# The gated linear recurrence ordered by halves of four heads, one VectorE multiply per level, constants staged in the 4 KB pool

## The chip, the core and the metric

The kernel runs on one core of a Trainium2 chip. The metric is the device time of one execution in microseconds (us). TensorE is called PE (its weight loads PEld), VectorE DVE, ScalarE ACT, GpSimd POOL, and SyncE SP.

## What is computed

A stack of three blocks over 256 rows of 1024 features in float32: an attention layer with a top-k mask (`dsa`) and a swiglu network, a gated linear recurrence (`hgrn`) and a swiglu network, and a third block. The change touches the recurrence. Cut to what matters:

```python
def hgrn2_mixer(x, lb, w_in, g_norm, w_o):
    q, f, i, g = split(x @ w_in)                 # four times 1024 columns, 8 heads of 128
    q = silu(q); fg = lb + (1 - lb) * sigmoid(f); k = 1 - fg; logf = log(fg)
    o = chunk_gated_linear(q, k, i, logf)        # S_t = diag(f_t) S_{t-1} + k_t v_t^T ; o_t = S_t^T q_t
    o = rms_norm(o, g_norm) * silu(g)
    return o @ w_o
```

## The kernel before

The 256 rows are two tiles of 128, t = 0 and 1. Every weight matrix is streamed once. SP loads a unit of 128 x 1024 numbers (512 KB) into one of 4 `raw` buffers, ACT rounds it to `rhi` (L174), DVE, or POOL for the keys in `ON_POOL`, takes the rest `rlo` (L176, L181), and a product is three matmuls (L210 to L212). One projection of 512 columns for one t is 24 matmuls of 128x512; its weights are four units, used for both t.

The strings `DSA`, `HEAD0` and so on, `HGRN` and `MIX` write out the order of the steps. A scheduler at build time takes that order as priorities and fixes each engine's own order from it, so instructions of neighbouring steps interleave. Each pool of buffers hands out whichever buffer is free.

In the first swiglu network (`ffn`), three small steps are laid beside chunks 2 and 3 (`ASIDE`). The last of them, `hgrn_consts` (L696), loads three constants over POOL's DMA queue into three tiles of the `raw` pool: `sel` (used by 8 matmuls at L705 to spread the bound `lb`), `lev` (the sums of the recurrence's levels, cast at L709), and `msk`, `suf`, `id64` together (cast or copied at L713 to L717). Their DVE, ACT and PE instructions are kept behind the work traced before them (`later`).

`hgrn` (L721): `project` (P.kind half.t) makes f, q, i, g by halves n of 512 columns, that is four heads. `evac` applies sigmoid, silu or a copy. `logs` (l.t) takes the logarithm over both halves, `turned` (t.t) turns q and k of all eight heads into `qT` and `kT`, `state` (S) builds the state that t = 1 reads. `pair` (p.t.i) does the recurrence of heads 2i and 2i+1 within 128 rows. It goes through 7 levels (8 for t = 1), two at a time: PE sums logarithms (L807, L808), ACT takes Exp (L810), then the late part of each block of rows is multiplied by q (L817) and the early part by k (L819; levels 2 and 5 on POOL, by `h_k2` and `h_k5`). PE multiplies them (L824, L830), and DVE copies the results by a mask (L835) into `blocks`, then into `attn` (L224). The output product is L846 and L848. Every second pair ends with `norm_heads` (L292 to L296). `gated` (g.t.n) multiplies by silu(g) and the norm's weight (L867 to L870) and turns the result; `out` (o.n.t) is the last projection, for which both halves of row tile t must be gated.

Pools named below: `w4` has 10 buffers of 4 KB per partition, `raw` 4, `rhi` and `rlo` 9 each. The logarithms lie in `rhi`/`rlo` tiles (`lfh`, `lfl`).

Of the kernel before, what the change touches and what calls it, by code (L numbers as in the profile page):

```python
# [10 lines left out]
F32 = mybir.dt.float32  # L11
F32R = mybir.dt.float32r
# [75 lines left out]
class Net:  # L88
# [631 lines left out]

    def hgrn(self, XT, dst):  # L721
        nc, ins = self.nc, self.ins
        w_in, w_o = ins["hgrn_w_in"][0], ins["hgrn_w_o"][0]
        lb, lev, msk, suf, id64, gn = self.hgrn_held
        fg, q, v, sg, qT, kT, lf, dg = ([None, None] for _ in range(8))

        def evac(kind, t, n, a):
            c = slice(n * 512, (n + 1) * 512)
            dst = {"f": fg, "q": q, "i": v, "g": sg}[kind]
            if n == 0:  # L730
                dst[t] = (self.g4 if kind in "ig" else self.w4)(name=kind)
            o = dst[t][:, c]
            if kind in "ig":
                self.copy(o, a, "h_" + kind)
            elif kind == "q":
                nc.scalar.activation(o, a, AF.Silu)
            else:

                nc.scalar.activation(o, a, AF.Sigmoid)
# [4 lines left out]
        def logs(t):  # L744

            lf[t] = (self.tile("rhi", (P, D), F32R, "lfh"), self.tile("rlo", (P, D), F32R, "lfl"))
            for n in range(2):
                c = slice(n * 512, (n + 1) * 512)
                x = self.w2(t, name="lf")
                nc.scalar.activation(x, fg[t][:, c], AF.Ln)  # L750
                self.halves(lf[t][0][:, c], lf[t][1][:, c], x)
                nc.vector.tensor_scalar(fg[t][:, c], fg[t][:, c], -1.0, 1.0, ALU.mult, ALU.add)

        def turned(t):

            dg[t] = self.sm(t, 8, name="dg")
            qT[t], kT[t] = self.w4((P, 8, P), name="qT"), self.w4((P, 8, P), name="kT")
            for n in range(2):
                c, b = slice(n * 512, (n + 1) * 512), slice(4 * n, 4 * n + 4)
                qk = self.w2(t, (P, 4, P), name="qk")  # L760
                nc.gpsimd.tensor_tensor(qk.rearrange("p h d -> p (h d)"), q[t][:, c], fg[t][:, c], ALU.mult)
                nc.vector.tensor_reduce(dg[t][:, b], qk, AX.X, ALU.add)
                self.copy(qT[t][:, b, :], self.blocksT(self.cols(q[t], 4 * n, 4), "hT"), "h_qT")
                self.copy(kT[t][:, b, :], self.blocksT(self.cols(fg[t], 4 * n, 4), "hT"), "h_kT")

        S = [None]

        def state():

            S[0] = self.w4((P, 8, P), name="S")  # L770
            for n in range(2):
                c = slice(n * 512, (n + 1) * 512)
                a = self.bank("hE")
                nc.tensor.matmul(a, suf, lf[0][0][:, c], start=True, stop=False)
                nc.tensor.matmul(a, suf, lf[0][1][:, c], start=False, stop=True)
                e = self.w2(0, name="e")
                nc.scalar.activation(e, a, AF.Exp)
                nc.vector.tensor_mul(e, e, fg[0][:, c])
                a = self.bank("hS", (P, 4, P))
                for j in range(4):  # L780
                    nc.tensor.matmul(
                        a[:, j, :], e[:, j * P : (j + 1) * P], v[0][:, n * 512 + j * P : n * 512 + (j + 1) * P],
                        start=True, stop=True,
                    )
                self.copy(S[0][:, n * 4 : n * 4 + 4, :], a, "h_S")

        part = lambda y, l, s: y.rearrange("p j (b s e) -> p j b s e", s=2, e=64 >> l)[:, :, :, s, :]

        def pair(t, i):

            hs = slice(2 * i, 2 * i + 2)
# [9 lines left out]
            for l0 in range(0, 7 + t, 2):  # L801
                m = min(2, 7 + t - l0)
                x = self.bank("hx%d" % (l0 // 2), (P, 2, 2, P), name="lx")
                rhs = lev[:, l0 * P : (l0 + m) * P].rearrange("p (l n) -> p l n", l=m)
                for j in range(2):
                    c = slice((2 * i + j) * P, (2 * i + j + 1) * P)
                    nc.tensor.matmul(x[:, j, :m, :], lf[t][0][:, c], rhs, start=True, stop=False)  # L807
                    nc.tensor.matmul(x[:, j, :m, :], lf[t][1][:, c], rhs, start=False, stop=True)  # L808
                e = self.w2(l0 // 2 % 2, (P, 2, 2, P), name="e")
                nc.scalar.activation(e[:, :, :m, :], x[:, :, :m, :], AF.Exp)  # L810
                for l in range(l0, l0 + m):
                    y = e[:, :, l - l0, :]
                    if l == 7:
                        nc.vector.tensor_mul(y, y, qT[t][:, hs, :])
# [28 lines left out]
            for j in range(2):  # L843
                h = 2 * i + j
# [29 lines left out]
        def out(n, t):
            if not rows:
# [429 lines left out]
MIX = (  # L1305
# [79 lines left out]
```

## Time and profile before

| | |
|---|---|
| median of 3 runs | 1156.86 us (1151.27 to 1157.37) |
| profiled execution, own time | 1154.16 us |
| its span | 1152.4 us |
| DMA | 187.33 MB, mean 163 GB/s |

Start times in all rows are us from the span's start. A window's row gives its length, then the busy time of each engine with its count of instructions, the granted clock of PE as a share of full speed (1.00 is 2.4 GHz, 0.50 is 1.2 GHz), the DMA engines' share, and GB/s. In a timeline, the bracket behind an instruction is how long its engine had been idle, and who ended that. Matmuls are pipelined, so the distance from one start to the next counts, not the length.

### The profile page before, as it was taken

To read this page: it belongs to the slowest core of one execution; us is meant where nothing else is said; L and a number is where in the kernel's file an instruction comes from. 1 tells how busy PE (TensorE), PEld (TensorE's weight loads), DVE (VectorE), ACT (ScalarE), POOL (GpSimd) and SP (SyncE) were. 2 spreads that over 40 slices of the span, in tenths; PEclk is the share of its full clock that TensorE was granted. 3 is DMA by queue.
4 is the path that set the end of the run, shared out by engine and by line. 5 is a ranking of instruction groups with operands and counts; after the bars stand their busy time and mean duration, and the time that the engine had idled before them with its cause. 6 is when DMAs were issued, how large, how long until landed. Compare 5 with 4: busy or idle time off the path is not lost.

```text
span 1152.4 us, 15343 instructions
## 1 busy us (share of the span) xinstructions
PE 1106.6 (96%) x5724; PEld 903.0 (78%) x5724; DVE 697.3 (61%) x1061; ACT 583.9 (51%) x832; POOL 224.3 (19%) x336
## 2 busy tenths in 40 slices
PE   8779999999999999999999999999999999999997
PEld 6546888878888777788888887887788878888886
DVE  6986755535566677875545486446655547454542
ACT  5656455525467466444444346763546456453441
POOL 2800620000432223200000022534100181000000
PEclk9989999999999899999999999999999999999999
DMA  8420756547445342365656545663554446566541
GB/s 250 159 85 5 243 166 229 182 119 255 146 146 173 103 145 77 119 214 180 218 183 192 175 131 174 207 159 102 164 192 146 146 146 225 174 222 202 171 140 37
DMA packets 98458, 187.33 MB, mean 163 GB/s; under 512 B 9400, under 2 KB 26952, under 8 KB 98384
## 3 DMA queue, kind: packets, MB, share of 16 engines
q1 hardware_dynamic: 94816, 176.28, 48.1%
q0 software_dynamic: 2864, 9.45, 2.5%
q8 instruction: 45, 0.74, 0.3%
q10 hardware_dynamic: 704, 0.62, 0.2%
q14 instruction: 29, 0.24, 0.1%
HBM read 185.28 MB, written 1.05 MB: 162 GB/s over the span
## 4 chain that ended last, share of the span: by engine, by line
PE 81%; DVE 8%; POOL 4%; DMA 3%; issue 2%; ACT 2%; SPq 0%; POOLq 0%; DVEq 0%; ACTq 0%
PE a L210 15%; PE a L211 15%; PE a L212 15%; PE y L211 8%; PE y L210 8%; PE y L212 8%; PE t L236 3%; POOL rlo L181 2%; DVE rlo L176 1%; PE lv L830 1%; DMA raw<-in_ffn_w_up_dram 1%; DMA raw<-in_ffn_w_gate_dram 1%; DVE m L381 1%; ACT rhi L174 1%; PE L L538 1%
## 5 line engine op out<-in xcount | busy, mean ns | idle before, releaser
L176 DVE TENSOR_TENSOR rlo<-raw,rhi 128x1024 fp32r<-128x1024 f32 (+4 forms) x306 | 370.2, 1215 | 216.3 <-ACT rhi L174 204.8
L174 ACT ACTIVATE rhi<-raw 128x1024 fp32r<-128x1024 f32 (+3 forms) x338 | 352.7, 1047 | 242.8 <-PE y L212 75.5
L210 PE MATMUL a<-rhi,xh 128*128 128x512 f32 (+4 forms) x840 | 318.6, 379 | 3.4 <-ACT sil L625 1.8
L211 PE MATMUL a<-rlo,xh 128*128 128x512 f32 (+4 forms) x840 | 316.7, 377 | 0.2 <-DVE rlo L176 0.2
L212 PE MATMUL a<-rhi,xl 128*128 128x512 f32 (+4 forms) x840 | 315.4, 376 | 0.0
L210 PEld LDWEIGHTS a<-rhi,xh 128*128 128x128 f32 x840 | 158.7, 189 | 32.1 <-ACT xh L174 2.0
L211 PEld LDWEIGHTS a<-rlo,xh 128*128 128x128 f32 x840 | 158.8, 189 | 27.8 <-DVE rlo L176 0.6
L212 PEld LDWEIGHTS a<-rhi,xl 128*128 128x128 f32 x840 | 158.8, 189 | 27.4
L181 POOL TENSOR_TENSOR rlo<-raw,rhi 128x256 fp32r<-128x256 f32 x128 | 99.2, 811 | 179.8 <-ACT rhi L174 179.7
L210 PE MATMUL y<-rhi,hth 128*128 128x512 f32 x264 | 104.7, 396 | 0.5 <-ACT hth L174 0.5
L212 PE MATMUL y<-rhi,htl 128*128 128x512 f32 x264 | 103.2, 391 | 0.0
L211 PE MATMUL y<-rlo,hth 128*128 128x512 f32 x264 | 102.9, 390 | 0.0
L210 PE MATMUL y<-rhi,xh 128*128 128x512 f32 (+2 forms) x152 | 59.1, 390 | 3.1 <-ACT rhi L174 3.1
L257 POOL TENSOR_SCALAR rv<-mv 128x1 f32<-128x1 f32 x10 | 7.2, 716 | 272.0 <-DVE mv L266 271.8
L211 PE MATMUL y<-rlo,xh 128*128 128x512 f32 (+2 forms) x152 | 59.0, 388 | 1.0 <-POOL rlo L181 0.6
L212 PE MATMUL y<-rhi,xl 128*128 128x512 f32 (+2 forms) x152 | 58.6, 387 | 0.0
L174 ACT ACTIVATE hth<-t 128x512 fp32r<-128x512 f32 (+1 forms) x36 | 20.1, 558 | 75.6 <-PE t L236 75.6
L210 PEld LDWEIGHTS y<-rhi,hth 128*128 128x128 f32 x264 | 49.6, 188 | 10.7 <-ACT hth L174 1.1
L212 PEld LDWEIGHTS y<-rhi,htl 128*128 128x128 f32 x264 | 49.5, 188 | 10.6
L211 PEld LDWEIGHTS y<-rlo,hth 128*128 128x128 f32 x264 | 49.6, 188 | 9.7
L631 DVE TENSOR_TENSOR sil<-a,sil 128x512 f32<-128x512 f32 (+1 forms) x36 | 23.2, 643 | 51.1 <-PE a L212 51.0
L625 ACT ACTIVATE sil<-a 128x512 f32<-128x512 f32 (+1 forms) x36 | 20.2, 561 | 58.9 <-PE a L212 58.8
(412 smaller groups left out, 1435.0 us busy)
## 6 DMA issues: line engine op xcount, KB each, us to landing
raw<-in_ffn_w_gate_dram SPq DMA_DIRECT2D x44, 512.0 KB, 4.7
raw<-in_ffn_w_up_dram SPq DMA_DIRECT2D x44, 512.0 KB, 4.7
raw<-in_ffn_w_down_dram SPq DMA_DIRECT2D x44, 512.0 KB, 4.6
raw<-in_hgrn_w_in_dram SPq DMA_DIRECT2D x32, 512.0 KB, 4.5
raw<-in_w_in_dram SPq DMA_DIRECT2D x24, 512.0 KB, 4.4
raw<-in_w_ffn_gate_dram SPq DMA_DIRECT2D x22, 512.0 KB, 4.3
raw<-in_w_ffn_up_dram SPq DMA_DIRECT2D x22, 512.0 KB, 4.6
raw<-in_w_ffn_down_dram SPq DMA_DIRECT2D x22, 512.0 KB, 4.5
```

What stands on the lines that cost most here:

```text
L174: self.nc.scalar.activation(hi, src, AF.Copy)
L176: self.nc.vector.tensor_sub(lo, src, hi.bitcast(F32))
L181: eng.tensor_sub(lo[:, c], src[:, c], hi[:, c].bitcast(F32))
L210: mm(out, xh, wh, start=start, stop=False)
L211: mm(out, xh, wl, start=False, stop=False)
L212: mm(out, xl, wh, start=False, stop=stop)
L236: self.nc.tensor.transpose(tp[:, j, :], b, self.ident)
L381: e2.tensor_tensor(m2, v[:, :, ::-1, :], s[:, None, :, :].to_broadcast(sh), ALU.mult)
L538: nc.tensor.matmul(L[:, j : j + 2, :], qT[t][:, g * 4 + (h0 + j) // 2, :], kT[:, g, :, :nk], start=False, stop=j == per - 2,)
L625: nc.scalar.activation(sil[ci, t][:, :cn], a[:, :cn], AF.Silu)
L631: nc.vector.tensor_mul(sil[ci, t][:, :cn], a[:, :cn], sil[ci, t][:, :cn])
L830: nc.tensor.matmul(lv[64 * c : 64 * c + 64, l - l0, j, :32], y, late, start=True, stop=True)
```

## The change

Five things are changed.

- `hgrn_consts` stages its three loads in tiles of `w4` instead of `raw`.
- f and q of one half and one t share a 4 KB tile, and so do the turned k and q (`QK[t, n]`, k first). `logs`, `turned` and `state` work on one half n, and the logarithms of one half, both t, lie in one `lfh`/`lfl` tile.
- In `pair`, each level has one DVE multiply over all 256 elements (two heads of 128): `asked(l)` is an access pattern over `QK` that takes k for the early and q for the late part of each block. The multiplies of levels 2 and 5 thereby leave POOL.
- `ON_POOL` loses `h_k2` and `h_k5`.
- The order `HGRN` goes through heads 0 to 3 for both t, then heads 4 to 7, with projections between the pairs.

```diff
-        raw = lambda: self.tile("raw", (P, 1024), F32, "raw")
-        sel = self.load(raw()[0:8, :], self.const("sel", 8)).rearrange("p (a b) -> p a b", a=8)
+        stage = [self.w4(name="stage") for _ in range(3)]
+        sel = self.load(stage[0][0:8, :], self.const("sel", 8)).rearrange("p (a b) -> p a b", a=8)
...
-        nc.vector.tensor_copy(lev, self.load(raw(), self.const("lev")))
+        nc.vector.tensor_copy(lev, self.load(stage[1], self.const("lev")))
...
-        both = self.load(raw()[:, : n + P + 64], self.consts[:, o : o + n + P + 64])
+        both = self.load(stage[2][:, : n + P + 64], self.consts[:, o : o + n + P + 64])
...
+                both = self.w4(name="fq")
+                fg[t, n], q[t, n] = both[:, :512], both[:, 512:]
...
+        def logs(t, n):
+            if n not in lf:
+                lf[n] = (self.tile("rhi", (P, 2, 512), F32R, "lfh"), self.tile("rlo", (P, 2, 512), F32R, "lfl"))
...
+        def turned(t, n):
...
+            both = QK[t, n] = self.w4((P, 2, 4, P), name="QK")
...
+            self.copy(both[:, 1, :, :], self.blocksT(self.cols(q[t, n], 0, 4), "hT"), "h_qT")
+            self.copy(both[:, 0, :, :], self.blocksT(self.cols(fg[t, n], 0, 4), "hT"), "h_kT")
...
+            def asked(l):
+                x = QK[t, n][:, 0, j0 : j0 + 2, :]
+                w = 64 >> l
+                return bass.AP(tensor=x.tensor, offset=x.offset, ap=[x.ap[0], [P, 2], [2 * w, 64 // w], [4 * P + w, 2], [1, w]])
...
-                    nc.vector.tensor_mul(part(y, l, 1), part(y, l, 1), part(qT[t][:, hs, :], l, 1))
-                    eng = nc.gpsimd if "h_k%d" % l in ON_POOL else nc.vector
-                    eng.tensor_tensor(part(y, l, 0), part(y, l, 0), part(kT[t][:, hs, :], l, 0), ALU.mult)
+                    y = y.rearrange("p j (b s e) -> p j b s e", s=2, e=64 >> l)
+                    nc.vector.tensor_tensor(y, y, asked(l), ALU.mult)
...
-    "b2_g0", "b2_kn", "b2_vm", "b2_w_out", "dsa_o", "h_d", "h_k2", "h_k5", "hgrn_f0", "hgrn_q1", "rk0b",
+    "b2_g0", "b2_kn", "b2_vm", "b2_w_out", "dsa_o", "h_d", "hgrn_f0", "hgrn_q1", "rk0b",
...
-    "P.f0.0 P.f1.0 Z P.f0.1 P.q0.0 P.q0.1 P.f1.1 P.q1.0 P.q1.1 l.1 l.0 t.0 P.i0.1 P.i0.0 P.i1.0 p.0.0 p.0.1 t.1 P.i1.1 "
-    "S P.g0.1 p.0.2 p.0.3 P.g0.0 p.1.0 p.1.1 g.0.0 p.1.2 p.1.3 P.g1.0 g.0.1 o.0.0 P.g1.1 g.1.0 o.1.0 g.1.1 o.0.1 n.0 "
-    "z.0 o.1.1 n.1"
+    "P.f0.0 P.f1.0 Z P.f0.1 P.f1.1 P.q0.0 P.q0.1 l.0.0 l.1.0 t.0.0 P.i0.0 P.i0.1 t.1.0 p.0.0 P.q1.0 p.0.1 S.0 P.q1.1 "
+    "p.1.0 P.i1.0 l.0.1 l.1.1 p.1.1 P.i1.1 t.0.1 t.1.1 p.0.2 P.g0.0 p.0.3 P.g0.1 S.1 p.1.2 P.g1.0 P.g1.1 g.0.0 p.1.3 "
+    "g.0.1 o.0.0 g.1.0 g.1.1 o.1.0 o.0.1 n.0 z.0 o.1.1 n.1"
```

## Rows read from the trace of the kernel before

**Rows 1.** From the page: busy time, share of the span and instructions of each engine, and the granted clock of PE in 40 slices.

```profile
PE 1106.6 (96%) x5724; PEld 903.0 (78%) x5724; DVE 697.3 (61%) x1061; ACT 583.9 (51%) x832; POOL 224.3 (19%) x336
...
PEclk9989999999999899999999999999999999999999
```

**Rows 2.** Windows of the first swiglu network, around the step that loads the constants.

```profile
230.00:240.00 10.00, 10.00 (x46) 8.29 (x45) 3.67 (x3) 3.24 (x4) 2.03 (x5) 1.00 0.48 131
240.00:250.00 10.00, 7.95 (x31) 6.18 (x30) 4.43 (x5) 2.72 (x3) 0.00 (x0) 0.83 0.22 59
...
275.00:280.00 5.00, 3.21 (x27) 3.01 (x26) 3.14 (x3) 3.25 (x5) 0.00 (x0) 1.00 0.75 252
...
243.00:247.00 4.00, 4.00 (x13) 3.27 (x14) 0.69 (x1) 1.21 (x2) 0.00 (x0) 0.57 0.46 135
```

**Rows 3.** Timeline of POOL in the same network: the loads of the three constants and what each had waited for.

```profile
225.39 0.56 POOL L152 DMA_DIRECT2D raw<-in_consts_dram  x1 [8.63 <-DVE rlo L176]
232.07 0.61 POOL L152 DMA_DIRECT2D raw<-in_consts_dram  x1 [6.12 <-DVE rlo L176]
233.44 0.55 POOL L152 DMA_DIRECT2D raw<-in_consts_dram  x1 [0.76 <-DVE rlo L176]
```

**Rows 4.** Timeline, same stretch: ACT's rounding of weight units and its releaser, and the matmuls and DVE copies that read the constants last.

```profile
240.01 1.06 ACT L174 ACTIVATE rhi<-raw 128x1024 fp32r<-128x1024 f32 x1 [5.93 <-DMA raw<-in_ffn_w_gate_dram]
...
246.39 1.06 ACT L174 ACTIVATE rhi<-raw 128x1024 fp32r<-128x1024 f32 x1 [2.03 <-DMA raw<-in_ffn_w_gate_dram]
...
252.47 1.06 ACT L174 ACTIVATE rhi<-raw 128x1024 fp32r<-128x1024 f32 x1
...
253.41 0.19 DVE L717 COPY id<-raw 128x64 f32<-128x64 f32 x1
...
259.97 2.05 PE L705 MATMUL t<-mx,raw 8*128 8x128 f32 x16
...
261.91 0.68 DVE L709 CAST lev<-raw 128x1024 fp32r<-128x1024 f32 x1
```

**Rows 5.** Windows of the recurrence, from the first pair to the last gate.

```profile
390.00:400.00 10.00, 8.85 (x71) 6.71 (x72) 6.23 (x18) 3.57 (x6) 2.78 (x4) 0.68 0.01 2
400.00:410.00 10.00, 9.25 (x53) 7.73 (x53) 8.17 (x16) 4.85 (x8) 5.62 (x8) 0.98 0.50 165
410.00:420.00 10.00, 9.77 (x76) 7.86 (x74) 3.83 (x13) 5.61 (x7) 0.62 (x1) 1.00 0.28 100
...
430.00:440.00 10.00, 8.46 (x80) 7.00 (x79) 8.74 (x24) 6.15 (x9) 4.63 (x7) 1.00 0.81 291
...
450.00:460.00 10.00, 9.44 (x91) 7.52 (x89) 7.48 (x23) 6.88 (x11) 5.45 (x11) 1.00 0.04 8
460.00:470.00 10.00, 9.23 (x88) 6.99 (x87) 8.60 (x25) 2.04 (x4) 2.43 (x3) 1.00 0.17 54
...
480.00:490.00 10.00, 9.45 (x48) 7.80 (x48) 8.84 (x13) 5.82 (x7) 2.37 (x3) 1.00 0.34 90
...
393.00:396.00 3.00, 3.00 (x31) 2.19 (x31) 1.49 (x9) 1.19 (x2) 0.00 (x0) 0.60 0.02 5
396.00:400.00 4.00, 4.00 (x20) 3.10 (x20) 1.77 (x5) 2.10 (x3) 0.00 (x0) 0.50 0.00 0
```

**Rows 6.** Instructions of the multiply lines: count, then shortest, median and longest duration in ns.

```profile
L817 DVE TENSOR_TENSOR e<-e,qT x56: 273/283/1255, 381.3 to 463.7; 128x128 f32<-128x128 f32 x56
...
L819 DVE TENSOR_TENSOR e<-e,kT x40: 273/283/1131, 381.5 to 464.1; 128x128 f32<-128x128 f32 x40
L819 POOL TENSOR_TENSOR e<-e,kT x16: 447/518/1765, 381.9 to 460.7; 128x128 f32<-128x128 f32 x16
```

**Rows 7.** Timeline of DVE within a pair: starts one after the other, halves of a level (L817, L819) and the whole level 7 (L814, 128x256).

```profile
440.07 0.41 DVE L814 TENSOR_TENSOR e<-e,qT 128x256 f32<-128x256 f32 x1
440.40 0.21 DVE L835 COPY_PREDICATED blocks<-msk,lv 128x64 f32<-128x64 uint8 x1
...
457.33 0.28 DVE L819 TENSOR_TENSOR e<-e,kT 128x128 f32<-128x128 f32 x1
457.53 0.29 DVE L817 TENSOR_TENSOR e<-e,qT 128x128 f32<-128x128 f32 x1
457.73 0.29 DVE L819 TENSOR_TENSOR e<-e,kT 128x128 f32<-128x128 f32 x1
```

**Rows 8.** Groups of ACT and POOL between 325 and 490 us by form: ACT's table loads, and the `rlo` that POOL makes in that stretch, of the q projection of heads 4 to 7 (`hgrn_q1`).

```profile
L810 ACT ACT_TABLE_LOAD x4 | 5.1, 1283 | 0.1
L867 ACT ACT_TABLE_LOAD x4 | 5.1, 1283 | 0.1
...
L181 POOL TENSOR_TENSOR rlo<-raw,rhi 128x256 fp32r<-128x256 f32 x16 | 11.6, 753 | 15.6 <-ACT rhi L174 15.5
```

**Rows 9.** The chain that ended last, in order of time, from the last pair to the last turned block: start, length, what.

```profile
466.04 0.38 PE lv L830 x8
...
467.41 1.29 DVE attn L224
...
468.73 1.94 DVE rlo L176 x2
...
478.45 2.24 POOL q L870
```

**Rows 10.** Timeline of PE at the end of the recurrence: the first and the last of the 24 matmuls of one output projection, and the transposes of the last gated half.

```profile
474.45 0.48 PE L210 MATMUL y<-rhi,oh 128*128 128x512 f32 x1
...
479.80 0.39 PE L212 MATMUL y<-rhi,ol 128*128 128x512 f32 x1
480.74 0.66 PE L236 MATMUL t<-ident,q 128*128 128x128 f32 x4 [0.55 <-POOL q L870]
```

More of the change, by code (lines that the diff above doesn't have):

```diff
@@ L724, in hgrn @@
         lb, lev, msk, suf, id64, gn = self.hgrn_held
-        fg, q, v, sg, qT, kT, lf, dg = ([None, None] for _ in range(8))
+        v, sg, dg = ([None, None] for _ in range(3))
+        fg, q, QK, lf = {}, {}, {}, {}
         def evac(kind, t, n, a):
             c = slice(n * 512, (n + 1) * 512)
[L729 to L732, printed above, removed]
             if kind in "ig":
-                self.copy(o, a, "h_" + kind)
+                dst = v if kind == "i" else sg
+                if n == 0:
+                    dst[t] = self.g4(name=kind)
+                self.copy(dst[t][:, c], a, "h_" + kind)
             elif kind == "q":
-                nc.scalar.activation(o, a, AF.Silu)
+                nc.scalar.activation(q[t, n], a, AF.Silu)
             else:
+                both = self.w4(name="fq")
+                fg[t, n], q[t, n] = both[:, :512], both[:, 512:]
+                o = fg[t, n]
                 nc.scalar.activation(o, a, AF.Sigmoid)
@@ L742, in evac @@
                 nc.vector.scalar_tensor_tensor(o, o, 2.0 ** -64, u, ALU.max, ALU.subtract)
[L744 to L764, printed above, removed]
@@ L766, in hgrn @@
-        S = [None]
[L768 to L785, printed above, removed]
+        def logs(t, n):
+            if n not in lf:
+                lf[n] = (self.tile("rhi", (P, 2, 512), F32R, "lfh"), self.tile("rlo", (P, 2, 512), F32R, "lfl"))
+            x = self.w2(t, name="lf")
+            nc.scalar.activation(x, fg[t, n], AF.Ln)
+            self.halves(lf[n][0][:, t, :], lf[n][1][:, t, :], x)
+            nc.vector.tensor_scalar(fg[t, n], fg[t, n], -1.0, 1.0, ALU.mult, ALU.add)
@@ new lines, in turned @@
+        def turned(t, n):
+            if n == 0:
+                dg[t] = self.sm(t, 8, name="dg")
+            both = QK[t, n] = self.w4((P, 2, 4, P), name="QK")
+            qk = self.w2(t, (P, 4, P), name="qk")
+            nc.gpsimd.tensor_tensor(qk.rearrange("p h d -> p (h d)"), q[t, n], fg[t, n], ALU.mult)
+            nc.vector.tensor_reduce(dg[t][:, 4 * n : 4 * n + 4], qk, AX.X, ALU.add)
+            self.copy(both[:, 1, :, :], self.blocksT(self.cols(q[t, n], 0, 4), "hT"), "h_qT")
+            self.copy(both[:, 0, :, :], self.blocksT(self.cols(fg[t, n], 0, 4), "hT"), "h_kT")
@@ new lines, in hgrn, with state @@
+        S = [None]
+        def state(n):
+            if n == 0:
+                S[0] = self.w4((P, 8, P), name="S")
+            a = self.bank("hE")
+            nc.tensor.matmul(a, suf, lf[n][0][:, 0, :], start=True, stop=False)
+            nc.tensor.matmul(a, suf, lf[n][1][:, 0, :], start=False, stop=True)
+            e = self.w2(0, name="e")
+            nc.scalar.activation(e, a, AF.Exp)
+            nc.vector.tensor_mul(e, e, fg[0, n])
+            a = self.bank("hS", (P, 4, P))
+            for j in range(4):
+                nc.tensor.matmul(
+                    a[:, j, :], e[:, j * P : (j + 1) * P], v[0][:, n * 512 + j * P : n * 512 + (j + 1) * P],
+                    start=True, stop=True,
+                )
+            self.copy(S[0][:, n * 4 : n * 4 + 4, :], a, "h_S")
@@ L787, in hgrn @@
         part = lambda y, l, s: y.rearrange("p j (b s e) -> p j b s e", s=2, e=64 >> l)[:, :, :, s, :]
         def pair(t, i):
-            hs = slice(2 * i, 2 * i + 2)
+            hs, n, j0 = slice(2 * i, 2 * i + 2), i // 2, 2 * (i % 2)
+            def asked(l):
+                x = QK[t, n][:, 0, j0 : j0 + 2, :]
+                w = 64 >> l
+                return bass.AP(tensor=x.tensor, offset=x.offset, ap=[x.ap[0], [P, 2], [2 * w, 64 // w], [4 * P + w, 2], [1, w]])
             b = self.w1(i % 2, (P, 2, 64), name="blocks")
@@ L805, in pair @@
                 for j in range(2):
-                    c = slice((2 * i + j) * P, (2 * i + j + 1) * P)
-                    nc.tensor.matmul(x[:, j, :m, :], lf[t][0][:, c], rhs, start=True, stop=False)
-                    nc.tensor.matmul(x[:, j, :m, :], lf[t][1][:, c], rhs, start=False, stop=True)
+                    c = slice((j0 + j) * P, (j0 + j + 1) * P)
+                    nc.tensor.matmul(x[:, j, :m, :], lf[n][0][:, t, c], rhs, start=True, stop=False)
+                    nc.tensor.matmul(x[:, j, :m, :], lf[n][1][:, t, c], rhs, start=False, stop=True)
                 e = self.w2(l0 // 2 % 2, (P, 2, 2, P), name="e")
@@ L813, in pair @@
                     if l == 7:
-                        nc.vector.tensor_mul(y, y, qT[t][:, hs, :])
+                        nc.vector.tensor_mul(y, y, QK[t, n][:, 1, j0 : j0 + 2, :])
                         continue
-                    nc.vector.tensor_mul(part(y, l, 1), part(y, l, 1), part(qT[t][:, hs, :], l, 1))
-                    eng = nc.gpsimd if "h_k%d" % l in ON_POOL else nc.vector
-                    eng.tensor_tensor(part(y, l, 0), part(y, l, 0), part(kT[t][:, hs, :], l, 0), ALU.mult)
+                    y = y.rearrange("p j (b s e) -> p j b s e", s=2, e=64 >> l)
+                    nc.vector.tensor_tensor(y, y, asked(l), ALU.mult)
                 lv = self.bank("hv%d" % (l0 // 2), (P, 2, 2, 64), name="lv")
@@ L849, in pair @@
             if i % 2:
-                self.norm_heads(t, self.ho, 4, P, q[t][:, (i // 2) * 512 : (i // 2 + 1) * 512])
+                self.norm_heads(t, self.ho, 4, P, q[t, n])
         groups, ys, rows, OT = {}, ([], []), [], [None, None]
@@ L867, in gated @@
             nc.scalar.activation(o, o, AF.Silu)
-            nc.vector.tensor_mul(q[t][:, c], q[t][:, c], o)
-            o3 = q[t][:, c].rearrange("p (h d) -> p h d", h=4)
+            nc.vector.tensor_mul(q[t, n], q[t, n], o)
+            o3 = q[t, n].rearrange("p (h d) -> p h d", h=4)
             nc.gpsimd.tensor_tensor(o3, o3, gn[:, None, :].to_broadcast([P, 4, P]), ALU.mult)
             b = slice(n * 4, n * 4 + 4)
-            self.splitT(q[t][:, c], OT[t][0][:, b, :], OT[t][1][:, b, :], 4, "hG")
+            self.splitT(q[t, n], OT[t][0][:, b, :], OT[t][1][:, b, :], 4, "hG")
         def out(n, t):
```

## The prediction

> **What bounds the kernel now.** I read the page's busy line first: PE is busy for 1106.6 of 1152.4 us, and no other engine is above 61% [rows 1]. The change removes no matmul, so it can win only where PE stands still or runs slowly. The granted clock over 40 slices is the second view. Past the start it dips in one slice only, the 14th, around 390 us [rows 1]. Then I went through PE's windows from the first swiglu network to the end of the recurrence, and two places stand out.
>
> The first is in the swiglu network, where the constants are loaded. From 230 to 240 us PE is busy all the time; from 240 to 250 us it is busy for 7.95 us, at a mean clock of 0.83; from 275 to 280 us for 3.21 us [rows 2]. The cause can be followed in three steps. POOL's three constant loads take a `raw` buffer each at 225, 232 and 233 us [rows 3]. Their last readers come at 253.4 us (`id64`), 259.97 to 262 us (`sel`) and 261.9 us (`lev`) [rows 4]. So for some 20 us the weights have one `raw` buffer out of four. In that time ACT can start a unit at 240.01, 246.39 and 252.47 us, the first two right behind a DMA [rows 4], a unit in about 6.2 us. PE uses one up much faster: 24 matmuls take 5.6 us (from the first start at 474.45 to the last at 479.80, plus one step [rows 10]), and four units serve two such projections, thus 2.8 us a unit. Three units at 3.4 us of deficit are 10 us, of which the units held ahead hide about half.
>
> The second place is the recurrence. From 390 us to 490 us the windows below 10.00 lose 1.15, 0.75, 0.23, 1.54, 0.56, 0.77 and 0.55 us, 5.55 us in all [rows 5]. From 393 to 400 us the clock is at 0.60 and 0.50, so 7 us of matmuls are worth 3.8: 3.2 us lost [rows 5]. That is where the order has two pairs and the turning of t = 1 with hardly a projection between them.
>
> **The change part by part.**
>
> **A, the staging.** With the constants in `w4`, all four `raw` buffers stay with the weights. What can be won is the idle time, 2.05 + 1.79 us, and the slow clock from 243 to 247 us, 4.00 x 0.43 = 1.7 us [rows 2]: 5.6 us. The 16 matmuls on `sel`, 2.05 us [rows 4], stay. The three loads keep POOL's queue and only lose their waits of 8.63, 6.12 and 0.76 us on a released `raw` buffer [rows 3]. Does `w4` have room? At that time it holds the two rows of the network's layer norm and the rotary table; with three stages, `lb` and `lev` that makes 8 of 10. In `hgrn` four f/q tiles, four QK tiles, the state and `lev` fill all 10, and by then `lb` is free, since the new order has P.f1.1 ahead of all turning. So I see no new wait. Bounds: 0 (the gap has another cause) to -5.6; I take -5.5, since all of rows 2 to 4 fit.
>
> **B, the order.** Before, the projections i1.1, g0.1, g0.0 and part of g1.0 lie between the first and the last pair; after, it is q1, i1, g0 and g1 for both t, eight of 5.6 us. PE has work of other steps to put wherever a pair waits for Exp, a multiply or a copy. At the best this gives back the slow clock (3.2 us) and the idle time ahead of the last pair (1.15 + 0.75 + 0.23 + 1.54 + 0.56 = 4.23 us): -7.4. At the worst it gives nothing, 0. I take the clock whole, because eight projections leave no stretch like 393 to 400 us, and half of the idle time, because pairs still start and end: -5.3.
>
> **C, the end of the recurrence.** What makes B pay takes cover from the end. From the last level's matmul at 466.04 us to the transposes of the last gated half at 480.74 us there are 14.7 us of chain: attn, the queue of `rlo` on DVE, the norm, the gate, POOL's multiply [rows 9, 10]. Before, the rest of g1.1 and of o.0.0 and the whole of o.1.0 lay beside it, and PE lost 0.77 + 0.55 us there [rows 5]. After, only o.0.0 and o.1.0 are independent of it, 11.2 us, and the first half of o.0.1 (four heads, 2.8 us). 14.7 - 11.2 = 3.5 us bare if that half isn't moved up, 0.7 if it is. Bounds: +5 (o.0.0 partly used up ahead of the last pair too) and -0.5 (a DVE queue that is shorter by then, where 1.94 us of `rlo` stand in the chain [rows 9]); I take +2.
>
> **D, the multiply.** Two halves of a level start 0.20 us apart, a whole 128x256 takes 0.33 us to the next start [rows 7]. 40 levels had both halves on DVE: 40 x (0.33 - 0.40) = -2.8 us. 16 had one on POOL: 16 x (0.33 - 0.20) = +2.1 us. DVE is 0.7 us better off, and POOL loses 16 multiplies of 518 ns median, 1765 at most [rows 6]. DVE isn't the bound, so this shortens waits already counted in B: 0 in the sum, -1 to +2 for the range. No row shows an access that goes from k to q and back at every element, as the last level's must; all halves, of whatever level, took 273 to 283 ns unless disturbed [rows 6].
>
> A rule that speaks against D: the Trainium skill, SBUF — State Buffer, section Door 1: The DMA port swizzle, says that SBUF is read in lines of 16 bytes and that full speed needs at least two accesses in a row to the same line. The last level changes line at every element, since k and q lie 2 KB apart. Where 128 more elements cost 0.13 us [rows 7], a second pass over 256 would cost 0.27 us, for 8 such multiplies an estimate of 2.1 us; by that rule the sum below would be 1147.5 instead of 1145.4 if all of it reached PE.
>
> **E, the tables.** ACT's table loads are 1283 ns each [rows 8]. In the new order the silu of q1 and the second pair of logarithms fall between pairs: some three more changes, 3.8 us on ACT, which is busy for 2 to 7 of every 10 us there [rows 5]. They lengthen a pair's wait for Exp, with projections as cover; without that cover, +3.8. I take 0. That k and q share tiles, and the turning by halves, change no instruction's size: 0.
>
> **Sum.** -5.5 - 5.3 + 2 = -8.8 us, against the profiled execution's 1154.2 us: 1145.4 us. The three runs shown have a median of 1156.86 us, 2.7 above that execution, and one at 1151.27, 2.9 below, so I take the profiled one as the middle, lean a little to the median, and forecast 1146 us. A measurement of this kernel can tell about 0.5% from no change, 5.8 us: faster means below 1151.1 us, slower above 1162.6.
>
> **The rivals.**
>
> 1. The end stands bare. The scheduler pulls o.0.0 into gaps ahead of the last pair. Then 5.6 us more of C's chain have no cover, and PE's clock falls behind such a gap as it did at 243 and 393 us [rows 2, 5], 3.2 us more: C is +10.8 instead of +2, and the kernel comes out at 1154 us, the same. For it: the order has nothing else ahead of p.1.3 but g1. Against it: eight projections are more than the pairs need.
>
> 2. The staging gap stays. If another thing starved the weights (the loads themselves, or the steps kept back on DVE), A is 0 and the time is 1154.2 - 3.3 = 1150.9 us. Against it: PE's gaps follow the `raw` buffers' hold to within some us [rows 3, 4].
>
> 3. POOL gets in DVE's way, and it is slower. q1's `rlo` pieces, 16 of 753 ns [rows 8], were made ahead of the pairs and now fall in among them. A multiply that takes 283 ns undisturbed took up to 1255 [rows 6]; if each of the 16 pieces stretches a multiply by 0.97 us, that is 15.5 us on DVE. It decides the sign only if nearly all of it reaches PE: 1145.4 + 15.5 = 1160.9 us, and with C's upper bound (+3) 1163.9. Against it: 16 multiplies leave POOL, and PE has projections as cover.
>
> **How the numbers follow.** Forecast 0.66, from 1138 (A and B whole, C at -0.5: 1140.7, and 2 to 3 us for pairs that get shorter through D) to 1151. Rival 1 0.18, rival 2 0.06, rival 3 0.10. The range of 8 in 10 leaves out the slower case and the far end of the forecast: 1138 to 1155. Faster takes the forecast but for its edge, and half of rival 2: 0.67. Same takes rival 1, the rest of rival 2 and the nearer outcomes of rival 3: 0.24. Slower 0.09.
>
> **What would show it.** A: windows around the constants' matmuls at 10.00 busy and clock 1.00, POOL's three loads without a wait for `rlo`, ACT's units no more 6 us apart. B: no window of the pairs under 1.00 in clock, idle time there under 3 us, `a` matmuls between `lv` matmuls all through. C: PE's idle time before the transposes of the last gated half, 1 to 4 us, released by POOL's `q` multiply. D: 56 multiplies of 128x256 starting 0.33 us apart at every level; at the last level 0.6 if the rule of the 16-byte lines holds. The forecast is wrong if the gap at the constants stays, if PE stands longer than 6 us behind the last pair, or if a new dip of the clock appears among the pairs.

## The result and the profile after

The changed kernel takes 1169.56 us (median of 4 runs, 1168.99 to 1170.37) against 1155.68 us for the kernel before on the same chip (4 runs): ratio 1.0116, 95% interval 1.0089 to 1.0143. It is slower, and lies outside the range of the prediction. Its profiled execution took 1170.37 us, its span is 1168.6 us. A trace shows one execution, and executions of one built kernel differ in their clock: all four of the kernel after have a mean granted clock of 0.980 to 0.982, while the ten of **e13** below go from 1152.03 us at 0.995, which is the traced one, to 1161.65 us at 0.982.

The page, busy line and granted clock, answering [rows 1]:

```profile
PE 1118.0 (96%) x5724; PEld 908.1 (78%) x5724; DVE 692.9 (59%) x1021; ACT 594.1 (51%) x840; POOL 214.1 (18%) x320
...
PEclk9989999999999979999999999999999999999999
```

The same 5724 matmuls keep PE busy for 11.4 us longer, in keeping with the lower clock below. The windows of the kernel after, first around the constants [rows 2], then in the recurrence [rows 5], and last the recurrence with all that lies around it:

```profile
240.00:250.00 10.00, 10.00 (x49) 8.08 (x49) 6.87 (x8) 5.45 (x6) 0.00 (x0) 1.00 0.50 161
...
260.00:270.00 10.00, 10.00 (x39) 8.08 (x38) 1.53 (x4) 2.70 (x3) 0.00 (x0) 0.85 0.34 120
...
360.00:370.00 10.00, 5.14 (x23) 4.26 (x22) 4.85 (x7) 4.51 (x6) 0.42 (x1) 0.83 0.75 263
...
380.00:390.00 10.00, 9.98 (x89) 7.75 (x89) 4.87 (x17) 3.51 (x7) 0.60 (x2) 1.00 0.00 0
...
400.00:410.00 10.00, 6.88 (x56) 5.69 (x56) 8.12 (x20) 9.10 (x12) 1.34 (x1) 0.99 0.19 56
410.00:420.00 10.00, 10.00 (x56) 6.94 (x56) 5.26 (x14) 2.71 (x3) 0.60 (x2) 0.50 0.14 35
...
430.00:440.00 10.00, 8.19 (x61) 5.47 (x62) 6.51 (x18) 0.51 (x2) 0.00 (x0) 0.69 0.71 225
...
490.00:500.00 10.00, 8.48 (x40) 6.76 (x39) 5.62 (x10) 2.26 (x3) 2.70 (x4) 1.00 0.19 53
...
300.00:510.00 210.00, 194.38 (x1222) 155.32 (x1221) 132.84 (x252) 115.57 (x147) 48.58 (x66) 0.94 0.36 117
```

In the same window of the kernel before PE is busy for 203.42 us at a mean clock of 0.98.

The staging gap is gone, as forecast. In the recurrence PE stands still for 15.6 us of 210 where it stood for 6.6, and the mean clock is 0.94 instead of 0.98, so 0.06 x 194 = 12 us of its busy time are lost. That is 9 us more of idle time and (as an estimate from these rounded clocks), with 0.02 x 203 = 4 us lost to the clock before, some 8 us more of slow clock. The clock is at 0.50 for all of 410 to 420 us, though PE is busy all the time: the stretch right behind the gaps of 400 to 410 us.

What PE waited for from 300 to 510 us in the kernel after (in total, times, longest). The lines are those of the kernel after: PE sums logarithms into `lx` (L814), ACT's Exp makes `e` of it (L817), DVE multiplies `e` (L825), PE multiplies the parts into `lv` (L830, L836), and POOL ends a gate at `fq` (L876). ACT's logarithm is L753, its silu L737 and L873.

```profile
PE lx L814 <- ACT QK L222: 4.9, 1, 4.9
PE lv L830 <- DVE e L825: 3.2, 2, 2.2
PE lx L814 <- ACT e L817: 2.6, 2, 2.2
PE t L236 <- POOL fq L876: 1.5, 1, 1.5
PE lv L836 <- DVE e L825: 1.3, 1, 1.3
```

In this list PE never waits for the weights of a projection. Its long waits are for the copies of the turned k and q, and for the pairs' own Exps and multiplies. Each of the three large waits can be followed in the timeline (all engines, kernel after):

```profile
355.63 4.79 POOL L181 TENSOR_TENSOR rlo<-raw,rhi 128x256 fp32r<-128x256 f32 x4
...
360.45 6.58 SPq L188 DMA_DIRECT2D raw<-in_hgrn_w_in_dram  x5
...
364.32 1.06 ACT L174 ACTIVATE rhi<-raw 128x1024 fp32r<-128x1024 f32 x1 [5.10 <-DMA raw<-in_hgrn_w_in_dram]
365.29 1.07 ACT L222 ACTIVATE QK<-t 128x512 f32<-128x512 f32 x2
365.92 0.58 PE L814 MATMUL lx<-lev,lfh 128*128 128x256 f32 x1 [4.86 <-ACT QK L222]
...
372.56 0.43 DVE L825 TENSOR_TENSOR e<-e,QK 128x256 f32<-128x256 f32 x1 [0.51 <-ACT e L817]
373.04 0.42 DVE L825 TENSOR_TENSOR e<-e,QK 128x256 f32<-128x256 f32 x1
373.79 0.50 DVE L825 TENSOR_TENSOR e<-e,QK 128x256 f32<-128x256 f32 x1 [0.20 <-ACT e L817]
...
396.50 1.28 ACT L753 ACT_TABLE_LOAD   x1
...
398.44 1.28 ACT L817 ACT_TABLE_LOAD   x1
...
400.23 0.62 ACT L174 ACTIVATE lfh<-lf 128x512 fp32r<-128x512 f32 x1
400.87 1.28 ACT L753 ACT_TABLE_LOAD   x1
...
404.17 1.99 ACT L174 ACTIVATE rhi<-raw 128x1024 fp32r<-128x1024 f32 x2
406.18 1.28 ACT L817 ACT_TABLE_LOAD   x1
407.47 1.09 ACT L817 ACTIVATE e<-lx 128x512 f32<-128x512 f32 x2
408.12 0.38 PE L814 MATMUL lx<-lev,lfh 128*128 128x256 f32 x1 [2.20 <-ACT e L817]
...
429.06 2.35 DVE L176 TENSOR_TENSOR rlo<-raw,rhi 128x1024 fp32r<-128x1024 f32 x2
431.33 1.43 DVE L825 TENSOR_TENSOR e<-e,QK 128x256 f32<-128x256 f32 x4
431.81 0.45 PE L830 MATMUL lv<-e 128*64 128x64 f32 x4 [2.21 <-DVE e L825]
...
496.11 0.66 PE L236 MATMUL t<-ident,fq 128*128 128x128 f32 x4 [1.52 <-POOL fq L876]
```

- Gap 1, 366 us: in ACT's order the rounding of a weight unit stands ahead of the copy of `QK`. The unit's DMA is late, so ACT idles for 5.10 us and the first pair with it. POOL's `rlo` pieces of q1, 4.79 us for one unit, hold a `raw` buffer just before: they end at 360.42 us, and SyncE's next load starts at 360.45.
- Gap 2, 401 and 408 us: four table loads of 1.28 us within 11 us, Ln, Exp, Ln, Exp, because the logarithms of heads 4 to 7 fall between Exps. Two units (404.17 us, 1.99 us) stand ahead of the last Exp as well.
- Gap 3, 432 us: two `rlo` of weight units stand ahead of the pair's multiplies on DVE.

ACT's table loads from 360 to 500 us, in the form of [rows 8]: 17, against 4 + 4 in the same stretch before.

```profile
L817 ACT ACT_TABLE_LOAD x9 | 11.5, 1283 | 0.2
L873 ACT ACT_TABLE_LOAD x4 | 5.1, 1283 | 0.1
L737 ACT ACT_TABLE_LOAD x2 | 2.6, 1283 | 0.0
L753 ACT ACT_TABLE_LOAD x2 | 2.6, 1283 | 0.0
```

And SyncE's longest wait from 330 to 470 us: the queue of the weight loads stood for 39.1 us, which is the 0.00 of DMA share in the window at 380 us. The second line is the kernel before in the same window.

```profile
SPq L188 <- DVE rlo L176: 87.5, 16, 39.1
...
SPq L188 <- DVE rlo L176: 93.7, 21, 35.8
```

So such a stop is not a loss by itself: the kernel before has one of 35.8 us, from 434 to 470 us, and PE stands for 2.9 us of that stretch.

### The profile page after: what moved, and what is told of

It reads as the page before. It is cut to its first block, busy times and chain, and to the rows that moved or that the text cites. A ratio compares the mean times of both kernels' runs of the same rounds, so it can differ in the third digit from the quotient of the medians.

```text
span 1168.6 us, 15281 instructions
## 1 busy us (share of the span) xinstructions
PE 1118.0 (96%) x5724; PEld 908.1 (78%) x5724; DVE 692.9 (59%) x1021; ACT 594.1 (51%) x840; POOL 214.1 (18%) x320
## 4 chain that ended last, share of the span: by engine, by line
PE 81%; DVE 7%; POOL 5%; ACT 3%; DMA 3%; issue 2%; SPq 0%; POOLq 0%; DVEq 0%; ACTq 0%
PE a L210 15%; PE a L212 15%; PE a L211 15%; PE y L210 8%; PE y L211 8%; PE y L212 8%; POOL rlo L181 3%; PE t L236 3%; PE lv L836 1%; DVE rlo L176 1%; DMA raw<-in_att_w_in_dram 1%; DVE m L381 1%; PE L L538 1%; PE o L1075 1%; ACT rhi L174 1%
## 5 line engine op out<-in xcount | busy, mean ns | idle before, releaser
L212 PE MATMUL a<-rhi,xl 128*128 128x512 f32 (+4 forms) x840 | 318.7, 380 | 0.0
```

Of the source, the lines that this page charges most:

```text
L212: mm(out, xl, wh, start=False, stop=stop)
```

## The experiments

Ratios are to the kernel before, run on the same chip, with 95% intervals. "us" below is a difference of ratios times 1155.7 us.

### Which part costs

**e1**: the kernel before with the three staging tiles of the diff, nothing else.

> The kernel before with only the three constants staged in the 4 KB pool. Theory (the new order costs, the staging wins): the gap at 240 to 250 us goes, 1155.7 - 4 = about 1151 to 1152 us. Rival (the staging gives its gain back, since the changed kernel shows a new dip of the clock to 0.85 at 260 to 270 us): 1154 to 1156 us.

1151.68 us, 0.9954 [0.9933, 0.9975]. A alone brings 5.3 us in the old order.

**e2**: the kernel after with the old order, spelled in the new steps (`l.t.n`, `t.t.n` and `S.n` are those steps for one half n).

```diff
-    "P.f0.0 P.f1.0 Z P.f0.1 P.f1.1 P.q0.0 P.q0.1 l.0.0 l.1.0 t.0.0 P.i0.0 P.i0.1 t.1.0 p.0.0 P.q1.0 p.0.1 S.0 P.q1.1 "
...
+    "P.f0.0 P.f1.0 Z P.f0.1 P.q0.0 P.q0.1 P.f1.1 P.q1.0 P.q1.1 l.1.0 l.1.1 l.0.0 l.0.1 t.0.0 t.0.1 P.i0.1 P.i0.0 P.i1.0 "
+    "p.0.0 p.0.1 t.1.0 t.1.1 P.i1.1 S.0 S.1 P.g0.1 p.0.2 p.0.3 P.g0.0 p.1.0 p.1.1 g.0.0 p.1.2 p.1.3 P.g1.0 g.0.1 o.0.0 "
...
```

> The changed kernel with the order of before written in its steps (l.1.0 l.1.1 l.0.0 l.0.1 and so on); staging, shared tiles and the one multiply per level stay. Theory (the order alone costs): the 14 us are gone, 1149 to 1153 us, and the idle time of PE between 300 and 510 us falls from 15.6 to 7 us or less. Rival (the wide multiply over k and q holds the pairs up): 1162 us or more.

1147.09 us, 0.9920 [0.9891, 0.9949]: faster than both kernels. Its windows of 300 to 510 us:

```profile
300.00:510.00 210.00, 206.75 (x1331) 167.87 (x1330) 150.45 (x273) 119.15 (x153) 48.69 (x65) 1.00 0.45 144
```

Idle time is 3.3 us, the clock 1.00. The new order alone costs 1.0116 - 0.9920, that is 22.6 us.

**e3**: the counterpart, the kernel after with the constants in `raw` again and two multiplies a level, levels 2 and 5 on POOL.

> The changed kernel with the constants staged in the raw pool again and two multiplies per level again (levels 2 and 5 of k on POOL): what is left of the change is the order and the shared tiles. Theory (the order costs): slower than the changed kernel by the lost staging gain, 1172 to 1176 us. Rival (the wide multiply costs): 1157 to 1162 us.

1171.28 us, 1.0136 [1.0106, 1.0167]. Without A and D the new order and the shared tiles cost 15.7 us against the kernel before. A and D together bring 2.3 us in the new order (after against e3, with intervals that overlap); in the old order A, D and the shared tiles bring 9.2 (e2 against the kernel before).

**e11**: e2 with two multiplies a level, as before.

```diff
-                    nc.vector.tensor_tensor(y, y, asked(l), ALU.mult)
+                    nc.vector.tensor_mul(part(y, l, 1), part(y, l, 1), part(qx, l, 1))
+                    eng = nc.gpsimd if "h_k%d" % l in ON_POOL else nc.vector
+                    eng.tensor_tensor(part(y, l, 0), part(y, l, 0), part(kx, l, 0), ALU.mult)
```

> The changed kernel in the order of before, with two multiplies per level again (levels 2 and 5 of k on POOL): the staging and the shared tiles are left. It prices the one multiply. Theory (it takes POOL's slow multiplies and a start of 0.07 us per level out of the pairs): 1150 to 1153 us, 3 to 6 us slower than with the one multiply. Rival (the multiply is worth nothing, the shared tiles are): 1146 to 1148 us.

1149.0 us, 0.9944 [0.9921, 0.9967]. The time lies between the two forecasts. One multiply is worth 2.8 us by the medians of the ratios, but the intervals overlap. In e11's trace the clock falls to 0.69 from 390 to 400 us, as in the kernel before [rows 5]; in e2's it doesn't. These traces are of executions of 1151.98 and 1144.75 us, so that this comes from the multiply isn't shown.

### What in the order costs

**e4**: q1's `rlo` on DVE instead of POOL (`hgrn_q1` out of `ON_POOL`).

> The changed kernel with the rest of q1's weights taken by DVE instead of POOL. Theory (a raw buffer held by POOL's slow pieces delays a weight unit that stands ahead of the turned k and q on ACT, 4.9 us idle on PE at 361 us): that gap goes, 1163 to 1165 us. Rival (the table loads between the pairs and the clock's dips behind them are the loss, POOL has no part): 1168 to 1170 us; or slower still, since DVE gets four units of 1.2 us more among the pairs.

1164.47 us, 1.0082 [1.0054, 1.0110]: gap 1 is gone, gap 3 stays (3.2 us on DVE's `e`). Worth 3.9 us, with intervals that overlap.

**e5**: 1 table load from 360 to 500 us in place of 17; **e12**: only the logarithms' ones taken out.

```diff
-                nc.scalar.activation(q[t, n], a, AF.Silu)
+                nc.scalar.activation(q[t, n], a, AF.Copy)
...
-            nc.scalar.activation(x, fg[t, n], AF.Ln)
+            nc.scalar.activation(x, fg[t, n], AF.Copy, scale=-0.01)
...
-            nc.scalar.activation(o, o, AF.Silu)
+            nc.scalar.activation(o, o, AF.Copy)
```

> The changed kernel with its silu of q and of g and its logarithm replaced by a copy on ACT (the logarithm by a copy times -0.01), so that the recurrence computes something else but needs hardly a table load; the order stays. Theory (17 table loads instead of 8 among the pairs delay Exp, PE waits in its fixed order and its clock falls): most of the 22 us go, 1150 to 1156 us. Rival (the order is bad by itself, through weight units and POOL ahead of what PE needs): 1163 us or more.

> The changed kernel with only the logarithm replaced by a copy times -0.01 on ACT (the recurrence computes something else); the steps l.0.1 and l.1.1 stay among the pairs with all their other instructions, and every silu stays. Theory (the table changes for the logarithms delay Exp between the pairs): 1153 to 1159 us. Rival (the other instructions of these steps in the queues of ACT and DVE are the loss): 1164 us or more.

e5: 1158.79 us, 1.0041 [1.0014, 1.0067], 8.7 us less than after; e12: 1164.80 us, 1.0066 [1.0041, 1.0091], 5.8 us less. e5 lies between its two forecasts, e12 in the range of its rival, and the interval of e12 just overlaps that of after. With nearly no table loads left the new order still is far from e2. In e12 gap 1 (4.8 us) and gap 3 (3.2 us) remain; in e5 they are 3.0 and 1.2 us, so that edit moved more than the tables.

**e6**: the second logarithms ahead of the pairs.

```diff
-... l.0.0 l.1.0 t.0.0 ... p.1.0 P.i1.0 l.0.1 l.1.1 p.1.1 ...
+... l.0.0 l.1.0 l.0.1 l.1.1 t.0.0 ... p.1.0 P.i1.0 p.1.1 ...
```

> The changed kernel with l.0.1 and l.1.1 moved up behind l.1.0, so that all logarithms are taken before the first pair; the output is the same. Theory (table loads): four loads fewer among the pairs, the waits of 1.3 and 2.2 us at 400 and 406 us and the clock's fall behind them go, 1161 to 1164 us. Rival (tables have no part): 1168 to 1172 us.

1152.97 us, 0.9986 [0.9969, 1.0003]: 15.0 us less than after and better than both forecasts, the largest single edit so far, where taking the logarithms' table loads away altogether gave 5.8 (e12). **e8** moves q1 ahead as well, **e9** is e6 with q1 on DVE.

> The changed kernel with q1's projections and all logarithms ahead of the first pair, still half by half: eight table loads and POOL's weight pieces leave the pairs, and two projections fewer lie between them. The output is the same. Theory (tables and POOL's pieces are the loss): 1150 to 1156 us. Rival (the halves by themselves, with the turning and the end bare, are the loss): 1160 us or more.

> The changed kernel with all logarithms ahead of the first pair and q1's weights on DVE instead of POOL; the output is the same. Theory (the two causes are separate: the logarithms among the pairs cost 17 us, POOL's pieces 5): 1147 to 1149 us, and the wait of PE for the turned k and q (2.5 us with the logarithms ahead) is gone. Rival (one cause, seen twice): 1152 to 1155 us, as with the logarithms ahead alone.

e8: 1156.40 us, 1.0015 [0.9985, 1.0044], no gain over e6. e9: 1153.52 us, 0.9971 [0.9954, 0.9989], in the range of its rival: with the logarithms ahead, q1 on DVE is worth 1.7 us, which the intervals can't tell from nothing.

### Why the logarithms' place costs so much

Their `lfh` and `lfl` tiles come from the pools `rhi` and `rlo`, 9 buffers each, that the weights fill. With those of heads 0 to 3 (one), q1's four units and i1's four, nine are taken (in the kernel after ACT rounds these eight units from 343.66 to 364.32 us). **e13** leaves every step where it is and only claims the second tiles with the first; **e14**, its control, puts the same two memsets on the first tiles, and claims nothing early.

```diff
-            if n not in lf:
-                lf[n] = (self.tile("rhi", (P, 2, 512), F32R, "lfh"), self.tile("rlo", (P, 2, 512), F32R, "lfl"))
+            if not lf:
+                for m in range(2):
+                    lf[m] = (self.tile("rhi", (P, 2, 512), F32R, "lfh"), self.tile("rlo", (P, 2, 512), F32R, "lfl"))
+                for x in lf[1]:
+                    nc.gpsimd.memset(x[:, 0, 0:1].bitcast(F32), 0.0)
```

> The kernel after with its order unchanged, the second pair of logarithms still between the pairs; only their two tiles (lfh, lfl of heads 4 to 7) are claimed together with those of heads 0 to 3, by a tiny POOL memset each, so that the weights never hold them. Theory of the buffers: what costs about 17 us at the logarithms' place (all steps as they are 1169.6, logarithms ahead 1153.0) is that lf, q1 and i1 together fill the 9 rhi and rlo buffers, so that the logarithms get theirs only once q1's weights are used up and the weights' DMA stops for nearly 40 us; with the tiles claimed early the logarithms come earlier, the stop of the DMA is shorter, and the time is 1153 to 1161 us. Theory of the place: the logarithms' ACT and DVE work stands late in those engines' order whatever buffers are free, the turned heads 4 to 7 come as late as before and the units behind crowd in; the time stays at 1164 to 1172 us.

> Control for the run with buffers claimed early: the same two tiny POOL memsets at the same place, but on the tiles of the first pair of logarithms (heads 0 to 3), which are claimed there anyway, so that nothing is claimed early and only the build-time schedule is disturbed. If the early claim itself gave the gain, this stays at 1166 to 1173 us like the kernel after. If the gain came from the shifted schedule and has nothing to do with the buffers, this one may come out anywhere, 1153 to 1161 us like the run before it.

e13: 1156.18 us, 1.0029 [1.0012, 1.0046]. e14: 1170.82 us, 1.0157 [1.0125, 1.0190]. The early claim gives back 10.1 us against after, 14.8 against its control. Windows of e13, then its waits of PE and of SyncE, then ACT's timeline (e13 to e16 have three lines more: L814, L817, L825, L830 and L876 are L817, L820, L828, L833 and L879 there):

```profile
360.00:370.00 10.00, 8.82 (x82) 6.89 (x82) 6.96 (x18) 6.32 (x9) 0.00 (x0) 1.00 0.62 209
...
380.00:390.00 10.00, 9.63 (x71) 7.88 (x70) 5.57 (x12) 8.32 (x11) 2.11 (x4) 1.00 0.50 157
...
410.00:420.00 10.00, 9.16 (x81) 7.21 (x79) 8.46 (x18) 6.16 (x11) 5.54 (x6) 1.00 0.86 262
```

```profile
PE lx L817 <- ACT QK L222: 1.2, 1, 1.2
...
PE lv L833 <- DVE e L828: 0.7, 2, 0.5
```

```profile
SPq L188 <- DVE rlo L176: 69.6, 18, 22.4
```

```profile
359.65 1.06 ACT L174 ACTIVATE rhi<-raw 128x1024 fp32r<-128x1024 f32 x1 [1.42 <-DMA raw<-in_hgrn_w_in_dram]
...
375.56 1.06 ACT L174 ACTIVATE rhi<-raw 128x1024 fp32r<-128x1024 f32 x1
...
392.64 0.62 ACT L174 ACTIVATE lfh<-lf 128x512 fp32r<-128x512 f32 x1
```

The weights move at 380 us (share 0.50 instead of 0.00), SyncE's longest wait falls from 39.1 to 22.4 us, the logarithms come 7.6 us earlier, and gaps 1 and 3 shrink from 4.9 and 3.2 to 1.2 and 0.7 us. The clock is at 1.00 in all these windows of e13's traced execution.

What the late claim held up was the next weights: in e13 ACT rounds units at 375.56, 379.28 and 381.87 us, where in the kernel after it rounds none between 364.32 and 402.70 us and then three in a row, among and right behind the logarithms. The runs e4, e5, e12 and e14, which all claim late, round no unit from 366 to 395 us either; e6 and e9, with the logarithms ahead, go on at 380.58 and 376.95 us. That the logarithms themselves waited for a buffer is not seen: ACT is not idle ahead of them in either trace, and the second pair's Exp comes 6.0 us earlier in e13 as well. Nor do they explain gap 1, which lies some 30 us ahead of them: there a weight unit is rounded at 359.65 instead of 364.32 us, so the early claim also changed the order of the units.

In e14 the waits are those of after:

```profile
PE lx L817 <- ACT QK L222: 5.2, 1, 5.2
PE lv L833 <- DVE e L828: 3.2, 2, 2.2
```

**e15**: e13 with q1 on DVE. **e16**: e15 without tables, by the edit of e5.

> Buffers claimed early as before, and the q projection of heads 4 to 7 split on DVE instead of POOL. If the two losses are separate (buffers about 13 us, POOL's hold on the raw buffers about 5), 1149 to 1153 us. If the early claim has already taken away the wait that POOL's pieces caused (PE's longest wait for a QK copy fell from 4.9 us to 1.2), there is nothing left for this edit: 1155 to 1158 us. Neither reaches the old order with the new multiply, 1147 us, since the table changes of ACT among the pairs are still there.

> The run before it (buffers claimed early, q1 split on DVE) with silu of q and g replaced by a copy and the logarithm by a copy times -0.01, as in the earlier runs without tables; so the recurrence computes something else, with the same instructions but for ACT's table loads. With both known losses gone the new order still stood at 1153.4 us, some 7 us above the old order with the new multiply. If ACT's table loads among the pairs are this rest, it falls to 1145 to 1149 us. If the rest is the late logarithms and the bare end of the recurrence, 1151 to 1155 us.

e15: 1153.39 us, 0.9988 [0.9966, 1.0009], 4.7 us less than e13, with intervals that don't overlap; it lies between its two forecasts. The trace shows only 1.2 us of it, the rest of gap 1, which is gone. So q1's pieces seem to be a loss of their own, but their price is 3.9 us in e4, 4.7 here, 1.7 in e9 and (below) 0.9 in e10, and it isn't told apart from what a shifted schedule does. e16: 1152.83 us, 0.9975 [0.9959, 0.9992]: once the other two are mended, the table loads are worth 1.5 us, which these intervals can't tell from nothing.

### The old order again

**e7**: e2 without tables. **e10**: e2 with q1 on DVE.

> The changed kernel in the order of before, with the same copies in place of silu and logarithm (the recurrence computes something else): the control for the run without tables in the new order. Theory: 8 loads fewer among the pairs, but PE waits there for 4 us in all, so 1143 to 1146 us. Rival (table loads cost PE about their own time everywhere): 1137 us or less.

> The changed kernel in the order of before, with q1's weights on DVE instead of POOL. Theory (in that order q1's pieces lie where neither DVE nor PE needs POOL): 1146 to 1149 us, no difference from the order of before. Rival (POOL's pieces hold the weights up in any order): 1142 to 1145 us, faster than every kernel so far.

e7: 1152.59 us, 0.9994 [0.9966, 1.0021], 8.6 us slower than e2 though ACT has less to do, and outside both forecasts. Its waits of PE show a gap that e2 doesn't have:

```profile
PE t L236 <- ACT QK L222: 2.1, 1, 2.1
```

Such an edit changes the scheduler's build-time order, and a unit came to stand ahead of a `QK` copy. From 300 to 510 us PE stands for 6.2 us against 3.3 in e2, so this is a part of the 8.6 us only; the rest isn't explained. So a difference of up to some 0.7% between two built schedules can't be given to one instruction alone. e10: 1146.53 us, 0.9912 [0.9879, 0.9946], the same as e2 within the intervals. e2 and e10 are the fastest versions; e1 and e11 beat both kernels too.

## Why the prediction was wrong

**A, right.** Forecast -5.5 us, e1 shows -5.3. A dip to 0.85 at 260 to 270 us took its place in part (in e1 it is there too, in e2 with the same staging it isn't). What makes it isn't shown; the last section has what PE did ahead of it.

**B, the step that failed.** "PE has work of other steps to put wherever a pair waits" gave -5.3 us with an end of 0. The order costs 22.6 us (e2 against after), C and E included. PE takes its instructions in a fixed order: where the next one is a pair's, no projection beside it goes ahead, as at 365.92, 408.12 and 431.81 us. I counted only what eight projections give to PE, and not what their 16 weight units ask of the pools, of SyncE's queue, of ACT and of DVE, right among the instructions that a pair waits for. From e10 up to the kernel after are 1.0116 - 0.9912, 23.6 us, in three steps:

| step | between | us |
|---|---|---|
| `lfh`, `lfl` of heads 4 to 7 claimed late (with most of gap 1) | after, e13 | 10.1 |
| q1's `rlo` on POOL, just ahead of the pairs | e13, e15 | 4.7 |
| the rest of the new order | e15, e10 | 8.8 |

That the early claim gives the first is shown by the control e14. How it reaches PE (late weights, then units and logarithms in a bunch on ACT and DVE) is read from the traces. The second is less than what e7 moved by. Of the rest, PE stands for 8.0 us of 300 to 510 us in e15 and for 2.9 in e10; among the waits that e10 doesn't have are that for the last gate (C) and those for Exp:

```profile
PE t L236 <- POOL fq L879: 1.5, 1, 1.5
...
PE lx L817 <- ACT e L820: 1.3, 2, 0.9
```

Why these waits come with the order stays open: e16 says that it is hardly tables, e9 (logarithms ahead, q1 on DVE, 0.9971) that it is hardly the logarithms' place alone, and 0.7% is also what e7 moved by.

**The clock, the wrong way.** I took the dip at 393 us as won. It went, but behind the larger gaps there are three new ones (360, 410 and 430 us): 8 us more lost, where 3.2 were to be won. The mean clock of 0.980 to 0.982 in all four executions says that this belongs to the changed kernel and not to the one execution traced. That "a new dip of the clock appears among the pairs" was named as what would prove the forecast wrong, without a price.

**C, right in kind, too large.** Forecast +2 us, 1 to 4 us idle before the last transposes, released by POOL. Measured 1.52 us behind POOL's `fq` at 496.11 us, 1.0 more than in [rows 10], and 0.2 more than the 0.77 + 0.55 us that the prediction counted behind the last pair.

**D, not told apart from the 0 that was taken.** The range was -1 to +2; -2.8 us in the old order (e11, e2) lies outside it by the medians, but the intervals overlap. The 56 multiplies have a median of 0.42 us. The rule of the Trainium skill (SBUF — State Buffer, section Door 1: The DMA port swizzle) that a change of the 16-byte line at every element costs speed, gave an estimate of 0.27 us more at the last level. The last multiply of the pair at 372 us takes 0.50 us instead of 0.42 or 0.43: 0.07 to 0.08 us for 256 elements. The rule's direction is there, not its size; eight of them make about 0.6 us.

**E, mis-sized.** "Some three more changes" are nine, 11.5 us on ACT. Without the logarithms' ones the kernel gains 5.8 us (e12), without all of them 8.7 (e5), and 1.5 once buffers and q1 are mended (e16), the first and the last not told apart from 0: the cover that I took for granted wasn't there in this schedule.

**The rivals.** Rival 3 named the right pieces with the wrong path: q1's pieces end at 360.42 us, and the first multiply at L825 starts at 368.29, so they stretch none. POOL's pieces hold a `raw` buffer, the next unit's DMA is late, and ACT, in order, makes the pair wait. By e4 and e15 they cost 4 to 5 us, not 15.5. The rival's own 1160.9 us lay below the 1162.6 from which the prediction counted slower, so of its 0.10 only the far end, with C at its bound, could stand behind the 0.09 for slower. No rival named the buffers of `lfh` and `lfl`, though the prediction counted `w4` for room: the same count for `rhi` and `rlo` (1 + 4 + 4 = 9) would have shown it.

## What to carry to other kernels

Where a step moves behind others, count the buffers of every pool that it claims, at its new place, against what the stream of weights holds there, and claim them before the stream runs ahead: here the early claim of two tiles was worth 10 us, while the same two tiny memsets without it were worth nothing (e14). Work laid beside a dependent chain covers a wait only where the fixed order of each engine has it ahead of the waiting instruction; its units in ACT's and DVE's queues lengthen the chain. Separate the parts of a change before judging it: staging, shared tiles and the one multiply together were worth keeping, in the old order, at 0.992. Give an edit that moves the schedule a control that moves it without the effect, as e14 does for e13.

## What the hardware showed unexpectedly

Behind the 3.1 us of idle time from 400 to 410 us the granted clock stayed at 0.50 (1.2 GHz) all the way from 410 to 420 us, with PE busy all the time (kernel after); in e13's traced execution, where PE stood for 0.84 us in the latter stretch, it was 1.00. From 300 to 510 us the slow clock cost nearly as much as the idle time itself. How much PE stands does not decide it alone: in the kernel after the 1.52 us lost from 490 to 500 us left the clock at 1.00, in the kernel before the 1.15 us lost from 390 to 400 us went with 0.68 [rows 5].

Nor do PE's own instructions alone. From 120 to 285 us they are the same, one for one, in the kernel after and in e2, and up to 259.4 us they start within 0.1 us of each other, with PE busy all the time from 240 us on. Then the clock falls in one and not in the other (kernel after, then e2):

```profile
260.00:262.00 2.00, 2.00 (x6) 1.56 (x5) 0.30 (x3) 0.00 (x0) 0.00 (x0) 0.50 1.04 350
...
260.00:262.00 2.00, 2.00 (x10) 1.66 (x9) 0.21 (x2) 0.00 (x0) 0.00 (x0) 1.00 0.96 331
```

From there to the first 128x256 product the same matmuls take 12.06 us (259.42 to 271.48) against 10.44 (259.33 to 269.77), 1.6 us more. What decides such a fall isn't shown, so one trace with a dip, or without, is weak evidence on a schedule.
